# Two projection stages of the first layer issued to TensorE in a written order

## The chip, the cores and the metric

One core of one Trainium2 chip runs the whole program in one launch. The metric is the device time of that launch in microseconds (us); lower is better.

## What is computed

Two blocks of two layers each work on 1024 latent tokens and 256 context tokens of width 1024. The change concerns the first layer of the first block, which mixes the tokens in two ways side by side: a Fourier mix, and attention whose queries and keys pass through small latents (MLA).

```python
def mla_q(q_a, q_norm, w_qb, rope):
    q = (rmsnorm(q_a, q_norm) @ w_qb).reshape(b, n, MLA_HEADS, MLA_NOPE + MLA_ROPE)
...
def mla_kv(kv_a, k_pe, kv_norm, w_kvb, rope):
    kv = (rmsnorm(kv_a, kv_norm) @ w_kvb).reshape(b, n, MLA_HEADS, MLA_NOPE + MLA_V)
...
def even_layer(h_lat, h_ctx, w_in, q_norm, w_qb, kv_norm, w_kvb, w_out, rope, ctx_out):
    f_in, f_gate, q_a, kv_a, k_pe, m_gate = split_cols(h_lat @ w_in, EVEN_SPLITS)
...
    y_l = jnp.concatenate([fourier_mix(f_in) * jax.nn.silu(f_gate),
                           a_l.reshape(b, n, MLA_WIDTH) * jax.nn.silu(m_gate)], axis=-1) @ w_out
```

The query latent `q_a` has 384 columns, the key latent `kv_a` 256, the rotated key part `k_pe` 32, the Fourier input `f_in` 512. Both latents pass a root-mean-square norm over their columns before they meet the next weight.

## The kernel before: tiles, stages and order

All 1280 tokens lie in three chunks (`CH`): 0 and 1 of 512 latent tokens, 2 of 256 context tokens. Each product is made of three matmuls in a fast float format, high part by high part, low by high, high by low; so every operand exists as a high and a low tile (names that end in h and l). A weight block is loaded by `wblk` in chunks (`wraw`, issued on SP), its high part made by ScalarE (L161) and its low part by GpSimd (L169). `proj` (L236) loops over chunks and blocks of 128 output columns; its matmuls are recorded on L212. `dense_tok` gives tiles of 128 tokens instead; its matmuls are recorded on L224.

The order of the work on each engine is set by a scheduler that plays the program through a cost model before it is built; each engine then works its list strictly in that order. `in_order()` pins the matmuls issued inside it to the order in which they are written; outside of it the scheduler may interleave them. `later()` gives work a low priority, so that it fills holes of that model.

The stage in question is the function `e1`, between about 95 and 297 us of the profile:

1. The key latent's first two chunks and four token tiles of `f_in` (`u`), then its chunk 2. `normed_split` (L591) takes each finished tile of sums out of PSUM in three readings: ScalarE makes the high part (L600), VectorE the low part (L601), ScalarE the squares (L389 for the first block of 128 columns, L391 for the others); GpSimd adds the squares into `acck` (L392).
2. `rstd_cols` (L356) sums the squares over the columns by matmuls with a column of ones (L361); VectorE turns the sums into reciprocal roots by nine small operations (L363, L347 to L354). `bcast_cols` (L366) spreads these over all partitions by matmuls (L372) that ScalarE copies out (L374). Before, both stand together in `rstd_bc`, behind the key latent's chunk 2.
3. The other token tiles of `u`: six of the first half, ten of the second, which also carry `k_pe`; VectorE copies that part into `kp` twice (L674, L675). Transposes of `kp` (L683) and VectorE's table products (L685 to L691) make the rotated key part.
4. The keys: 12 tiles, each scaled out of PSUM by VectorE (L699). The values: 10 tiles, taken out by ScalarE.
5. The query latent: three blocks of 128 columns over three chunks (180 units of a 512-column matmul in all, a matmul of 256 columns counted as half a unit), into `accq`; then the sums and the spreading of all ten columns (`rstd_bc`), then the queries, 18 tiles of nine matmuls, scaled by VectorE (L728).
6. The Fourier mix (L834 on), whose VectorE part `fourier_in` (L799) is issued before the query latent: 18 additions on VectorE (L806 to L822) and 4 on GpSimd over ten `u` tiles, which SP loads back from memory.

Beside all of that runs `mod_rest` (L458) under `later()`: 32 loads (`wmt`, 512 KB each, two buffers) on SP, and on VectorE one or two products `wmj` (L477) per load. Its pool lies where the Fourier tiles go later, so SP's loads of the ten `u` tiles wait for the last `wmj`. Two gate tiles (24 matmuls each into the PSUM bank `f`) fill TensorE before the Fourier mix; VectorE's step on them is recorded on L385. PSUM has seven working banks (two `s`, one `o`, three `p`, one `g`) and the bank `f` for norms and gates.

Of the kernel before, what the change touches and what calls it, by code (L numbers as in the profile page):

```python
# [15 lines left out]
ALU = mybir.AluOpType  # L16
# [26 lines left out]
class Kern:  # L43
# [77 lines left out]
    def stg(self, n=512):  # L121
        return self.t(self.gp_, [P, 512], tag="stg", bufs=4)[:, 0:n]
# [497 lines left out]
    def e1(self):  # L620
        nc, A, V = self.nc, self.A, self.nc.vector
# [20 lines left out]
        KV = Act(2)  # L642
# [22 lines left out]
        for b, n in ((0, 256), (1, 288)):  # L665
            w = self.wblk(w_in, b * 256, n, pool=kvp) if b else wu
            for j in (0, 1, 2, 3, 8, 9, 4, 5, 6, 7) if b else (4, 5, 6, 7, 8, 9):
# [8 lines left out]
        for c, (a, b) in enumerate(CH):  # L676
            tab = self.t(kvp, [32, 2, 512], tag="kpe_tab", bufs=1)
            if c < 2:
                self.dma(tab, A["kpe_tab"][:, :, a:b])
            for e in range(2 if c < 2 else 1):  # L680
                s = self.sps()
                for j in range(a // P, b // P):
                    nc.tensor.transpose(s[0:32, j * P - a:j * P - a + P], kp[:, j, 32 * e:32 * e + 32], self.ident)  # L683
                if c == 2:
                    V.tensor_copy(kpe[:, a:b], s[0:32, 0:b - a])  # L685
                elif e == 0:
                    V.tensor_tensor(kpe[:, a:b], s[0:32], tab[:, 0], ALU.mult)
                else:
                    o = stg()[0:32]
                    V.tensor_tensor(o, s[0:32], tab[:, 1], ALU.mult)  # L690
                    V.tensor_tensor(kpe[:, a:b], kpe[:, a:b], o, ALU.add)  # L691
        self.dma(kpe_scr, kpe)
        w_kvb, w_qb = A["e_w_kvb"], A["e_w_qb"]
        w = self.wblk(w_kvb, 0, 512)

# [5 lines left out]
        self.proj(w, [(i * P, P, i) for i in range(4)], KV, ALLC, k_evac)  # L701
# [16 lines left out]
        w = self.wblk(w_in, 1056, 256)  # L718
# [24 lines left out]
        gs = self.open("e1g", side="right")  # L743
        gate, mix, todo = self.gate_evac(gate_scr, None, gs, 2), Act(), []
# [5 lines left out]
        def fill():  # L750
# [6 lines left out]
            for c in ALLC:  # L757
                for w, i in W:
                    yield from gates(w, i, c)
                todo.extend((k, c) for k in range(8))  # L760

# [22 lines left out]
        f, before = fill(), 0  # L784
# [1388 lines left out]
```

## Time and profile before

| | us |
|---|---|
| median of 3 runs | 2573.57 |
| lowest, highest | 2561.18, 2574.37 |
| the profiled execution | 2567.91 |
| its span in the trace | 2566.1 |

| engine | busy us | share of the span |
|---|---|---|
| TensorE (PE) | 2422.8 | 94% |
| VectorE (DVE) | 1685.4 | 66% |
| ScalarE (ACT) | 1127.3 | 44% |
| GpSimd (POOL) | 890.6 | 35% |

A busy share is an average over stages with different limits. PE is the engine to look at first, and the 6% of the span in which it does nothing are where an order can matter, together with the stretches in which its granted clock is at the half level after a pause.

### The profile page before, as it was taken

The numbers are of one execution on the slowest core, as the hardware profiler recorded it, in microseconds if no ns is written. First come the engines' busy times: TensorE is split into PE (matmuls) and PEld (weight loads), VectorE is DVE, ScalarE is ACT, GpSimd is POOL, SyncE is SP. The second block draws the span as 40 slices with busy tenths as digits, with TensorE's granted clock in tenths as the row PEclk, the third lists the DMA queues.
The fourth block names the chain that finished last, engine by engine and source line by source line (L and its number), as shares of the span: only waits on it lengthen the run. The fifth ranks groups of instructions, "written<-read, shape, count | busy, mean of one in ns | idle before, by whom it ended". The sixth has DMA issues, their size and how long they took to land. (4 is left out here: it accounts for less than half of the span.)

```text
span 2566.1 us, 36049 instructions
## 1 busy us (share of the span) xinstructions
PE 2422.8 (94%) x12814; PEld 1958.0 (76%) x12814; DVE 1685.4 (66%) x2983; ACT 1127.3 (44%) x2201; POOL 890.6 (35%) x750
## 2 busy tenths in 40 slices
PE   5999999999999999999898999999999999999998
PEld 3887777777678876766666779887877777799888
DVE  6785437788755648777776373547888577773455
ACT  3413226666652325655565233345655333513331
POOL 4204243354411152332322124145452243453231
PEclk7999999999999999999999999999999999999999
DMA  7476431132324231222323423233333332201433
GB/s 238 140 217 202 156 107 53 52 102 73 93 78 144 91 94 52 69 77 65 95 71 111 134 96 89 90 108 100 90 103 124 100 109 89 73 18 54 168 103 103
DMA packets 217092, 265.16 MB, mean 103 GB/s; under 512 B 42768, under 2 KB 142768, under 8 KB 216784
## 3 DMA queue, kind: packets, MB, share of 16 engines
q1 hardware_dynamic: 216192, 262.75, 32.9%
q8 instruction: 101, 1.65, 0.3%
q14 instruction: 79, 0.65, 0.1%
q10 hardware_dynamic: 720, 0.10, 0.0%
HBM read 188.60 MB, written 71.97 MB: 102 GB/s over the span
## 5 line engine op out<-in xcount | busy, mean ns | idle before, releaser
L169 POOL TENSOR_TENSOR wlo<-wraw,whi 128x512 fp32r<-128x512 f32 (+3 forms) x229 | 314.4, 1385 | 602.9 <-ACT whi L161 522.6
L169 DVE TENSOR_TENSOR pl<-pf,ph 128x512 fp32r<-128x512 f32 (+1 forms) x328 | 257.8, 787 | 80.3 <-ACT pf L957 41.0
L161 ACT ACTIVATE whi<-wraw 128x512 fp32r<-128x512 f32 (+3 forms) x261 | 154.5, 613 | 333.9 <-DMA wraw<-in_even_w_in 40.1
L957 ACT ACTIVATE ph<-s 128x512 fp32r<-128x512 f32 (+1 forms) x176 | 101.4, 576 | 107.4 <-PE s L954 106.7
L919 DVE TENSOR_REDUCE mx<-p 128x1 f32<-128x512 f32 (+1 forms) x208 | 116.8, 575 | 35.4 <-PE p L918 34.2
L1255 ACT ACTIVATE ph<-s 128x512 fp32r<-128x512 f32 x152 | 90.7, 597 | 107.6 <-PE s L1247 58.2
L212 PE MATMUL s<-ah,whi 128*128 128x512 f32 (+1 forms) x328 | 130.8, 399 | 5.6 <-ACT ah L493 3.2
L212 PE MATMUL s<-al,whi 128*128 128x512 f32 (+1 forms) x328 | 129.1, 394 | 1.8 <-DVE al L495 1.4
L212 PE MATMUL s<-ah,wlo 128*128 128x512 f32 (+1 forms) x328 | 129.4, 394 | 0.0
L212 PE MATMUL g<-ah,whi 128*128 128x512 f32 (+1 forms) x312 | 122.4, 392 | 3.4 <-DVE mixg L385 3.4
L212 PE MATMUL f<-ah,whi 128*128 128x512 f32 x304 | 123.7, 407 | 1.3 <-DVE stg L1368 0.8
L212 PE MATMUL f<-al,whi 128*128 128x512 f32 x304 | 123.0, 405 | 0.0
L212 PE MATMUL f<-ah,wlo 128*128 128x512 f32 x304 | 122.9, 404 | 0.0
L212 PE MATMUL g<-ah,wlo 128*128 128x512 f32 (+1 forms) x312 | 121.5, 390 | 0.0
L212 PE MATMUL g<-al,whi 128*128 128x512 f32 (+1 forms) x312 | 121.5, 390 | 0.0
L1621 DVE TENSOR_TENSOR_SCAN scu<-scu,ones_col 128x128 f32<-128x128 f32 (+3 forms) x64 | 97.1, 1531 | 14.1 <-ACT scu L1617 12.5
L1215 DVE CUSTOM_DVE_ANT_0 p<-p,maskt 128x384 f32<-128x384 f32 (+1 forms) x128 | 67.4, 530 | 58.0 <-PE p L1214 58.0
L957 ACT ACTIVATE pf<-s 128x512 f32<-128x512 f32 (+1 forms) x176 | 100.9, 573 | 2.0 <-DVE pl L169 1.8
L477 DVE CUSTOM_DVE_ANT_0 wmj<-wmt,srow,c_b_mod 128x1024 bf16<-128x1024 f32 x56 | 76.7, 1370 | 30.0 <-DMA wmt<-in_w_modT 27.7
L1255 ACT ACTIVATE pf<-s 128x512 f32<-128x512 f32 x152 | 90.2, 593 | 0.1
L212 PE MATMUL p<-ah,whi 128*128 128x512 f32 x224 | 89.5, 401 | 0.4 <-DVE x L1338 0.4
L212 PE MATMUL p<-al,whi 128*128 128x512 f32 x224 | 89.7, 400 | 0.0
(777 smaller groups left out, 7617.0 us busy)
## 6 DMA issues: line engine op xcount, KB each, us to landing
wmt<-in_w_modT SPq DMA_DIRECT2D x32, 512.0 KB
wraw<-in_even_w_in SPq DMA_DIRECT2D x56, 256.0 KB
wraw<-in_odd_w_in SPq DMA_DIRECT2D x48, 256.0 KB
wraw<-in_o_w_in SPq DMA_DIRECT2D x40, 256.0 KB
xold<-x_scr SPq DMA_DIRECT2D x40, 256.0 KB
mraw<-in_w_mod SPq DMA_DIRECT2D x16, 512.0 KB
x_scr<-x SPq DMA_DIRECT2D x32, 256.0 KB
mixx<-m_scr SPq DMA_DIRECT2D x30, 256.0 KB
```

Of the source, the lines that this page charges most:

```text
L161: nc.scalar.activation(out=out, in_=in_, func=AF.Copy)
L169: return e.tensor_tensor(out, in_, hi.bitcast(F32), ALU.subtract)
L212: self.nc.tensor.matmul(out, ws[:, k, c:c + m], a[k][ch], start=first and i == j == 0, stop=last and i == len(ks) - 1 and j == 2)
L477: V.tensor_tensor_reduce(out=junk, in0=w, in1=s[:, i], scale=0.5, scalar=self.bm[l][:, m, i:i + 1], op0=ALU.mult, op1=ALU.add, accum_out=s ...
L919: V.reduce_max(mx[:, e, j:j + 1], d[:, 0:y - x], axis=AX)
L957: nc.scalar.activation(out=t, in_=s, func=AF.Exp, scale=MLA_SCALE)
L1215: V.tensor_tensor_reduce(out=d[:, 0:n], in0=d[:, 0:n], in1=self.mask[:, off:off + n], scale=1.0, scalar=-3.0e38, op0=ALU.add, op1=ALU.max, ...
L1255: nc.scalar.activation(out=t, in_=s, func=AF.Exp, scale=0.125)
L1621: V.tensor_tensor_scan(out=rev, data0=rev, data1=self.ones.to_broadcast([P, n]), initial=1.0, op0=ALU.mult, op1=ALU.mult)
```

## The change

Key latent: the sums of the norm follow three token tiles of `u` later than they did, the spreading follows seven tiles behind the sums, and the transposes of `kp` are spread over the key tiles, two after each chunk. Everything from the first token tile to the last transpose is pinned in the written order.

Query latent: the third block of 128 columns (`w2`) no longer follows all of the first two but comes chunk by chunk, and its weights are loaded into the query pool. The norm is made chunk by chunk as well, with sums and spreading apart from each other and other matmuls between them; so there are three chains of nine small VectorE operations in place of one. The queries follow in pinned order, the third pair of blocks as before. The generator of the gate tiles is created earlier.

```diff
-        self.proj(wk, ((0, P, 0), (P, P, 1)), act, (2,), ev)
...
-        self.rstd_bc(rkb, acc, TT, 256.0, rkt)
...
+        with self.in_order():
+            u_proj(wu, 0, 256, (4,))
+            self.proj(wk, ((0, P, 0), (P, P, 1)), act, (2,), ev)
+            u_proj(wu, 0, 256, (5, 6))
+            self.rstd_cols(acc, TT // P, 256.0, rkt)
+            u_proj(wu, 0, 256, (7, 8, 9))
+            wu = self.wblk(w_in, 256, 288, pool=kvp)
+            u_proj(wu, 1, 288, (0, 1, 2, 3))
+            self.bcast_cols(rkt, TT // P, rkb)
+            u_proj(wu, 1, 288, (8, 9, 4, 5, 6, 7))
...
-        self.proj(w, [(i * P, P, i) for i in range(4)], KV, ALLC, k_evac)
+        with self.in_order():
+            for c in ALLC:
+                self.proj(w, [(i * P, P, i) for i in range(4)], KV, (c,), k_evac)
+                next(turns)
+                next(turns, None)
+            for _ in turns:
+                pass
...
         w = self.wblk(w_in, 1056, 256)
-        self.proj(w, ((0, P, 0), (P, P, 1)), act, ALLC, ev)
-        w = self.wblk(w_in, 1312, 128)
-        self.proj(w, ((0, P, 2),), act, ALLC, ev)
+        w2 = self.wblk(w_in, 1312, 128, pool=qp)
         rqb = acc
-        self.rstd_bc(rqb, acc, TT, 384.0)
+        first = {}
...
-        first = {}
-        for i in (4, 0, 2):
+        r = {c: self.t(qp, [P, (CH[c][1] - CH[c][0]) // P], nm=f"rq{c}") for c in ALLC}
+
+        def sums(c):
+            a, b = CH[c]
+            self.rstd_cols(acc[:, a:b], (b - a) // P, 384.0, r[c])
+
+        def spread(c):
+            a, b = CH[c]
+            self.bcast_cols(r[c], (b - a) // P, rqb[:, a:b])
+        first2, third = ((0, P, 0), (P, P, 1)), ((0, P, 2),)
+        with self.in_order():
+            self.proj(w, first2, act, (0,), ev)
+            self.proj(w2, third, act, (0,), ev)
+            self.proj(w, first2, act, (2,), ev)
+            sums(0)
+            self.proj(w2, third, act, (2,), ev)
+            self.proj(w, first2, act, (1,), ev)
+            spread(0)
+            sums(2)
+            self.proj(w2, third, act, (1,), ev)
+            spread(2)
+            w4 = self.wblk(w_qb, 4 * P, 256)
+            self.proj(w4, ((0, P, 4), (P, P, 5)), Q, (0,), q_evac)
+            sums(1)
+            self.proj(w4, ((0, P, 4), (P, P, 5)), Q, (2,), q_evac)
+            w0 = self.wblk(w_qb, 0, 256, pool=qp)
+            self.proj(w0, ((0, P, 0), (P, P, 1)), Q, (0, 2), q_evac)
+            spread(1)
+            self.proj(w4, ((0, P, 4), (P, P, 5)), Q, (1,), q_evac)
+            self.proj(w0, ((0, P, 0), (P, P, 1)), Q, (1,), q_evac)
+        for i in (2,):
```

Outside this stage the lists of all engines stay as they were but for single neighbours. What the scheduler makes of the change is seen at three places.

The first is on VectorE where the second half of `u` ends and the keys begin: the copies of `kp`, `mod_rest`'s products `wmj` (an ISA row each, with the read of its sum behind it) and the first scaled key tile. Before (L674 and L675 copy, L699 scales):

```order
L674 COPY kp_265_1094<-p_302_1551 128x32
L675 COPY kp_265_1094<-p_302_1551 128x32
L690 TENSOR_TENSOR stg_307_1594<-p_306_1589,kpe_tab_304_1581 32x512
L477 ISA wmj_194_620,mod1_110<-wmt_213_699,srow_192_618,c_b_mod1_614 128x1024
L477 ISA mod1_110 128x1
L685 COPY kpe_228_760<-s_313_1614 32x256
L691 TENSOR_TENSOR kpe_228_760<-kpe_228_760,stg_307_1594 32x512
L477 ISA wmj_194_620,mod1_110<-wmt_213_699,srow_192_618,c_b_mod1_614 128x1024
L477 ISA mod1_110 128x1
L687 TENSOR_TENSOR kpe_228_760<-g_309_1599,kpe_tab_308_1597 32x512
L690 TENSOR_TENSOR stg_311_1610<-s_310_1605,kpe_tab_308_1597 32x512
L699 TENSOR_TENSOR stg_319_1636<-o_318_1629,rkb_258_1055 128x512
```

With the change (L672 and L673 copy, L711 scales):

```order
L672 COPY kp_251_993<-o_300_1521 128x32
L673 COPY kp_251_993<-o_300_1521 128x32
L477 ISA wmj_194_620,mod1_110<-wmt_213_699,srow_192_618,c_b_mod1_614 128x1024
L477 ISA mod1_110 128x1
L477 ISA wmj_194_620,mod1_110<-wmt_214_703,srow_192_618,c_b_mod1_614 128x1024
L477 ISA mod1_110 128x1
L477 ISA wmj_194_620,mod1_110<-wmt_214_703,srow_192_618,c_b_mod1_614 128x1024
L477 ISA mod1_110 128x1
L672 COPY kp_251_993<-p_302_1551 128x32
L673 COPY kp_251_993<-p_302_1551 128x32
L711 TENSOR_TENSOR stg_309_1598<-p_308_1591,rkb_250_992 128x512
```

The last copy of `kp` and the first key tile stood behind the products of load 213 (the first key tile) and 212 (the copy); both now stand behind those of load 214, and the table products come after the first keys.

The second is on VectorE where `mod_rest` ends and `fourier_in` begins (fa and u tiles). Before:

```order
L601 SCALAR_TENSOR_TENSOR ql01_405_2088<-s_403_2062,c_e_q_norm_752,qh01_404_2087 128x512
L477 ISA wmj_194_620,mod1_110<-wmt_226_744,srow_192_618,c_b_mod1_614 128x1024
L477 ISA mod1_110 128x1
L601 SCALAR_TENSOR_TENSOR ql11_409_2119<-s_407_2093,c_e_q_norm_752,qh11_408_2118 128x512
L806 TENSOR_TENSOR fa0_376_1884<-u0_366_1864,u4_370_1868 128x512
L806 TENSOR_TENSOR fa1_377_1885<-u1_367_1865,u5_371_1869 128x512
L807 TENSOR_TENSOR u4_370_1868<-u0_366_1864,u4_370_1868 128x512
L806 TENSOR_TENSOR fa2_378_1886<-u2_368_1866,u6_372_1870 128x512
L807 TENSOR_TENSOR u5_371_1869<-u1_367_1865,u5_371_1869 128x512
L806 TENSOR_TENSOR fa3_379_1887<-u3_369_1867,u7_373_1871 128x512
L807 TENSOR_TENSOR u6_372_1870<-u2_368_1866,u6_372_1870 128x512
L601 SCALAR_TENSOR_TENSOR ql20_423_2185<-o_421_2159,c_e_q_norm_752,qh20_422_2184 128x512
```

With the change, at the end of `fourier_in` (L852 to L868 now), where the chain that makes chunk 0's reciprocal roots `rq0` (L363, L347 to L354) runs through it:

```order
L861 TENSOR_TENSOR fa1_377_1885<-u0_366_1864,u1_367_1865 128x512
L863 TENSOR_TENSOR fa3_379_1887<-u5_371_1869,u7_373_1871 128x512
L350 SCALAR_TENSOR_TENSOR rq0_397_1970<-rs_t_422_2138,rq0_397_1970 128x4
L865 SCALAR_TENSOR_TENSOR u0_366_1864<-fa2_378_1886,u4_370_1868 128x512
L866 SCALAR_TENSOR_TENSOR u1_367_1865<-fa2_378_1886,u4_370_1868 128x512
L867 SCALAR_TENSOR_TENSOR u5_371_1869<-fa3_379_1887,u6_372_1870 128x512
L868 SCALAR_TENSOR_TENSOR u7_373_1871<-fa3_379_1887,u6_372_1870 128x512
L351 TENSOR_TENSOR rs_t_422_2138<-rq0_397_1970 128x4
L601 SCALAR_TENSOR_TENSOR ql01_429_2205<-o_427_2179,c_e_q_norm_752,qh01_428_2204 128x512
L352 TENSOR_TENSOR rs_t_422_2138<-rs_t_422_2138,rs_s_421_2136 128x4
L353 SCALAR_TENSOR_TENSOR rs_t_422_2138<-rs_t_422_2138 128x4
L354 SCALAR_TENSOR_TENSOR rq0_397_1970<-rs_t_422_2138,rq0_397_1970 128x4
```

Before, no step of the norm stood among `fourier_in`'s; now `rq0` is finished three places behind its last addition. The third block's low part for chunk 0 (`ql20`), which stood eight places into `fourier_in`, now stands ahead of it.

The third is on SP, where the third block's weights (`wraw`, 128 columns, eight chunks of 64 KB in all) and `mod_rest`'s last loads alternate. Before:

```order
L128 DMA wmt_222_732<-in_w_modT 128x1024
L128 DMA wraw_417_2143<-in_e_w_in 128x128
L128 DMA wmt_223_735<-in_w_modT 128x1024
L128 DMA wraw_418_2147<-in_e_w_in 128x128
L128 DMA wraw_419_2151<-in_e_w_in 128x128
L128 DMA wmt_224_738<-in_w_modT 128x1024
L128 DMA wraw_420_2155<-in_e_w_in 128x128
L128 DMA wmt_225_741<-in_w_modT 128x1024
L128 DMA wraw_442_2296<-in_e_w_qb 128x256
L128 DMA wraw_443_2300<-in_e_w_qb 128x256
L128 DMA wmt_226_744<-in_w_modT 128x1024
```

With the change:

```order
L128 DMA wraw_391_1946<-in_e_w_in 128x128
L128 DMA wraw_392_1950<-in_e_w_in 128x128
L128 DMA wmt_224_738<-in_w_modT 128x1024
L128 DMA wmt_225_741<-in_w_modT 128x1024
L128 DMA wraw_393_1954<-in_e_w_in 128x128
L128 DMA wraw_394_1958<-in_e_w_in 128x128
L128 DMA wmt_226_744<-in_w_modT 128x1024
L128 DMA wraw_395_1962<-in_e_w_in 128x128
L128 DMA wraw_396_1966<-in_e_w_in 128x128
L128 DMA wraw_446_2300<-in_e_w_qb 128x256
L128 DMA u0_366_1864<-u_scr_73 128x512
```

The third block's last chunk still stands next to load 226, the last of `mod_rest`, though the block itself is now wanted right behind the first two blocks of chunk 0.

## Rows read from the trace of the kernel before

**Rows 1.** Windows: busy time of each engine in two stretches of the stage.

```profile
core 0: us, PE busy (x) PEld busy (x) DVE busy (x) ACT busy (x) POOL busy (x), PEclk, DMA share, GB/s
95.00:182.00 87.00, 80.13 (x582) 76.35 (x581) 74.01 (x134) 19.47 (x41) 16.05 (x9) 0.98 0.65 202
...
240.00:290.00 50.00, 44.09 (x220) 37.43 (x220) 31.94 (x48) 8.78 (x19) 24.77 (x21) 0.90 0.37 118
```

**Rows 2.** Waits of PE from 95 to 345 us: total, times, longest.

```profile
PE f L361 <- POOL accq L392: 4.9, 1, 4.9
PE f L372 <- DVE rkt L354: 3.1, 1, 3.1
PE f L212 <- DVE gst L385: 2.3, 1, 2.3
PE g L683 <- DVE kp L674: 1.7, 1, 1.7
...
PE p L212 <- DVE kpe L687: 1.3, 1, 1.3
PE f L372 <- ACT accq L374: 0.7, 1, 0.7
```

**Rows 3.** Windows again: the three stretches at the half clock.

```profile
132.20:135.60 3.40, 3.40 (x16) 3.40 (x17) 2.69 (x6) 0.60 (x1) 0.00 (x0) 0.50 0.86 261
241.40:251.70 10.30, 7.50 (x23) 6.34 (x24) 10.30 (x12) 2.52 (x6) 8.47 (x7) 0.50 0.18 51
292.60:296.00 3.40, 3.40 (x19) 3.40 (x18) 0.00 (x0) 0.00 (x0) 0.00 (x0) 0.50 0.94 336
```

**Rows 4.** Timeline of DVE, 165 to 188 us: start, length, instruction, idle before.

```profile
165.92 1.28 DVE L477 CUSTOM_DVE_ANT_0 wmj<-wmt,srow,c_b_mod 128x1024 bf16<-128x1024 f32 x1 [0.25 <-DMA wmt<-in_w_modT]
...
169.06 0.17 DVE L674 COPY kp<-p 128x32 f32<-128x32 f32 x1
...
174.40 0.67 DVE L699 TENSOR_TENSOR stg<-o,rkb 128x512 f32<-128x512 f32 x1
...
187.60 0.68 DVE L699 TENSOR_TENSOR stg<-g,rkb 128x512 f32<-128x512 f32 x1
```

**Rows 5.** Timeline of SP's queue: two loads of mod_rest, then the u tiles.

```profile
162.23 0.33 SPq L128 DMA_DIRECT2D wmt<-in_w_modT  x1
...
221.94 0.38 SPq L128 DMA_DIRECT2D wmt<-in_w_modT  x1
227.60 4.71 SPq L128 DMA_DIRECT2D u<-u_scr  x10
```

**Rows 6.** Timeline of DVE, 226 to 257 us.

```profile
226.28 1.28 DVE L477 CUSTOM_DVE_ANT_0 wmj<-wmt,srow,c_b_mod 128x1024 bf16<-128x1024 f32 x1 [2.31 <-DMA wmt<-in_w_modT]
...
233.68 1.29 DVE L806 TENSOR_TENSOR fa<-u,u 128x512 f32<-128x512 f32 x2 [5.44 <-DMA u<-u_scr]
234.90 0.68 DVE L807 TENSOR_TENSOR u<-u,u 128x512 f32<-128x512 f32 x1
...
239.01 0.74 DVE L601 SCALAR_TENSOR_TENSOR ql<-o,c_e_q_norm,qh 128x512 fp32r<-128x512 f32 x1
...
244.62 1.21 DVE L816 TENSOR_TENSOR fa<-u,u 128x512 f32<-128x512 f32 x1
...
251.52 0.74 DVE L601 SCALAR_TENSOR_TENSOR ql<-p,c_e_q_norm,qh 128x512 fp32r<-128x512 f32 x1
257.06 0.17 DVE L363 TENSOR_SCALAR rs_s<-f 128x10 f32<-128x10 f32 x1 [4.81 <-PE f L361]
```

**Rows 7.** Timelines of PE, four rows from 195 to 297 us.

```profile
195.78 0.39 PE L212 MATMUL p<-ah,whi 128*128 128x512 f32 x1
...
237.80 0.39 PE L212 MATMUL p<-qh,whi 128*128 128x512 f32 x1
...
244.20 1.23 PE L361 MATMUL f<-ones_col,accq 128*128 128x1 f32 x5 [4.86 <-POOL accq L392]
...
296.41 0.67 PE L846 MATMUL o<-c_f_tw,fa 128*128 128x256 f32 x2
```

More of the change, by code (lines that the diff above doesn't have):

```diff
@@ L659, in e1, with u_proj @@
             self.dma(u_scr[j * 256:(j + 1) * 256, 0:256].rearrange("(e p) n -> p e n", p=P), t.rearrange("p (e n) -> p e n", e=2))
-        self.proj(wk, ((0, P, 0), (P, P, 1)), act, (2,), ev)
         rkt = self.t(kvp, [P, 10], nm="rkt")
         rkb = self.t(kvp, [P, TT], nm="rkb")
-        self.rstd_bc(rkb, acc, TT, 256.0, rkt)
         kp = self.t(kvp, [P, 10, 64], nm="kp")
-        for b, n in ((0, 256), (1, 288)):
-            w = self.wblk(w_in, b * 256, n, pool=kvp) if b else wu
-            for j in (0, 1, 2, 3, 8, 9, 4, 5, 6, 7) if b else (4, 5, 6, 7, 8, 9):
+        def u_proj(w, b, n, js):
+            for j in js:
                 s = self.sps()[:, 0:n]
@@ L675, in e1 @@
                     V.tensor_copy(kp[:, j, 32:64].rearrange("p (a b) -> p a b", a=2), s[:, 256:288].rearrange("p (a b) -> p a b", a=2)[:, ::-1, :])
[L676 to L691, printed above, removed]
@@ L692, in e1, with rotate_kpe @@
-        self.dma(kpe_scr, kpe)
+        def rotate_kpe():
+            for c, (a, b) in enumerate(CH):
+                tab = self.t(kvp, [32, 2, 512], tag="kpe_tab", bufs=1)
+                if c < 2:
+                    self.dma(tab, A["kpe_tab"][:, :, a:b])
+                for e in range(2 if c < 2 else 1):
+                    s = self.sps()
+                    for j in range(a // P, b // P):
+                        nc.tensor.transpose(s[0:32, j * P - a:j * P - a + P], kp[:, j, 32 * e:32 * e + 32], self.ident)
+                    if c == 2:
+                        V.tensor_copy(kpe[:, a:b], s[0:32, 0:b - a])
+                    elif e == 0:
+                        V.tensor_tensor(kpe[:, a:b], s[0:32], tab[:, 0], ALU.mult)
+                    else:
+                        o = stg()[0:32]
+                        V.tensor_tensor(o, s[0:32], tab[:, 1], ALU.mult)
+                        V.tensor_tensor(kpe[:, a:b], kpe[:, a:b], o, ALU.add)
+                    yield
+            self.dma(kpe_scr, kpe)
@@ L694, in e1 @@
         w = self.wblk(w_kvb, 0, 512)
+        turns = rotate_kpe()
         def k_evac(i, c, ps):
@@ L717, in e1, with gates, fill @@
         ev = self.normed_split(qp, "q", Q, gq, acc, sm)
+        gate = self.gate_evac(gate_scr)
+        def gates(w, i, c):
+            for e in (0, 1):
+                yield from self.dense_steps(w, e * P, act, c, self.FT, lambda ps: gate(i + e, c, ps))
+        def fill():
+            for i, c0 in ((0, 544), (2, 800)):
+                w = self.wblk(w_in, c0, 256)
+                for c in ALLC:
+                    yield from gates(w, i, c)
+            W = [(self.wblk(w_in, c0, 256), i) for i, c0 in ((4, 1696), (6, 1952))]
+            for c in ALLC:
+                for w, i in W:
+                    yield from gates(w, i, c)
+                todo.extend((k, c) for k in range(8))
+        f, before = fill(), 0
         w = self.wblk(w_in, 1056, 256)
-        self.proj(w, ((0, P, 0), (P, P, 1)), act, ALLC, ev)
-        w = self.wblk(w_in, 1312, 128)
-        self.proj(w, ((0, P, 2),), act, ALLC, ev)
+        w2 = self.wblk(w_in, 1312, 128, pool=qp)
         rqb = acc
-        self.rstd_bc(rqb, acc, TT, 384.0)
+        first = {}
         def q_evac(i, c, ps):
@@ L744, in e1 @@
         gate, mix, todo = self.gate_evac(gate_scr, None, gs, 2), Act(), []
-        def gates(w, i, c):
-            for e in (0, 1):
-                yield from self.dense_steps(w, e * P, act, c, self.FT, lambda ps: gate(i + e, c, ps))
-        def fill():
-            for i, c0 in ((0, 544), (2, 800)):
-                w = self.wblk(w_in, c0, 256)
-                for c in ALLC:
-                    yield from gates(w, i, c)
-            W = [(self.wblk(w_in, c0, 256), i) for i, c0 in ((4, 1696), (6, 1952))]
[L757 to L760, printed above, removed]
         def add():
@@ L783, in e1 @@
         am_scr = dram("am_scr", [512, TT])
-        f, before = fill(), 0
         with self.later():
```

## The prediction

> **What bounds the kernel now.** TensorE (PE) is busy for 94% of the span, so a change of order can win back only its waits and the stretches at the half clock. I read the waits of PE over the stage first. Those that the new order can reach are two for sums or roots of a norm, 4.9 and 3.1 us, two around the rotated key part, 1.7 and 1.3, and one for a spread, 0.7 [rows 2]: 11.7 us. Then I read the granted clock. Behind the wait of 3.1 us lie 3.4 us at 0.50, which is 1.2 GHz, all busy; around that of 4.9 us the clock is 0.50 for 10.3 us, of which PE worked 7.5 [rows 3]. Work at the half level takes twice its time, so the loss is 1.7 and 3.75 us. Together that is 17.1 us, the most the change can give.
>
> The windows then show who else is busy. From 95 to 182 us VectorE (DVE) worked 74.0 of 87 us, from 240 to 290 us 31.9 of 50 [rows 1]. So in the first part PE's order is not free: DVE has to follow. The timeline of DVE says what sets its pace. A `mod_rest` load issued at 162.23 [rows 5] is used at 165.92 [rows 4], 3.7 us later, and its two products take 1.3 us each. With two buffers, and each load issued once the products on its buffer are over, two loads go through per 3.7 + 2.6 = 6.3 us. The copies of `kp` and the keys stand in the same list, at fixed places among these products.
>
> **Key part.** Work on PE and the other engines stays the same; only places change. The waits of 3.1 (with 1.7 of clock), 1.7 and 1.3 us go: -7.8 us on PE. But PE's gain there is not kept. Before, the first key tile on DVE followed load 213 and ran at 174.40 [rows 4], with most of the rotation done. Now it follows load 214. Load 212 is used at 165.92, so by the pace above 214 is used at 172.2 and its products end at 174.9; with two copies the first key runs at about 175.2, however early PE is. PE then fills the seven PSUM banks and waits. From first to last key DVE took 13.9 us (174.40 to the end of the row at 187.60). Now the whole rotation stands behind the first key too: four table products of about 0.6 us and a copy of 0.35 that used to come before, 2.75 us, and two products of 1.3. So the last key ends at about 194.5 in place of 188.3, 6 us later, and the query latent starts on PE at about 202 in place of 195.78 [rows 7]. The bounds: 196 if the keys don't hold PE at all, 206 if PE adds a wait of its own at the sums, whose last square now has GpSimd's weight split ahead of it; I take 202, as it follows from the list.
>
> The Trainium skill, page "DMA: Bandwidth & Descriptors", section "Anatomy of one DMA — SWDGE (gpsimd) path", gives 2.0 us and the bytes at 436 GB/s, for a load from another queue than ours; for 512 KB that would be an estimate of 3.2 us. The row has 3.7 us, so here the trace differs; by 3.2 us the pace would be 0.5 us quicker per two loads, and the last of `mod_rest` about 3 us earlier.
>
> **Query part, what goes.** Before, PE waited 4.9 us for GpSimd's last squares, because the third block's low part `ql20` stood eight places into `fourier_in`, which itself waited for the `u` tiles until 233.68; `ql20` came at 239.01 [rows 6]. In the new list it stands ahead, so this wait goes with its clock loss: -8.6 us, and -0.7 for the spread.
>
> **Query part, what comes.** PE needs `rq0` for the first spread. The third block, chunk 0, comes right behind the first two, but SP sends its last chunks beside load 226. The 180 units took 42.0 us (195.78 to 237.80, [rows 7]), 0.233 each; the third block's chunk 0 could end 72 units on, at 218.8, its last weights are in at about 221: a wait of about 2.5 us. At 156 units, 36.4 us, plus 0.5 for four sums, PE reaches the spread at about 241.
>
> On DVE `rq0` ends behind `fourier_in`, and that waits for the `u` tiles. The last `wmj` ended 53.2 us behind the first key (174.40 to 227.56, [rows 4, 6]), 13 loads. Now 12 are left. At the quick pace, 3.2 us a load, with 4 us of rotation beside, that is 42 us, with nothing gained 53; I take the middle, 48, so the last `wmj` is over at 223 (217 to 228). From there to `fourier_in` it was 6.1 us (227.56 to 233.68); `fourier_in` with two low parts took 17.8 us (233.68 to 251.52, [rows 6]). Now there are three low parts and nine small steps in it, of 0.17 us each by the row at 257.06: 19.4 us. So `rq0` is ready at 223 + 6.1 + 19.4 = 248.5 (242.5 to 254). PE waits there some 7 us: the old wait comes back at another matmul. The 18 further small steps of the other chains, 3 us, lie beside matmuls, since DVE is idle for 18 of 50 us in that stretch [rows 1]; without this cover the next spreads would be 3 us later.
>
> **The sum.** From 237.80 to the Fourier mix at 296.41 PE took 58.6 us [rows 7]. Without the waits of 4.9, 0.7 and 2.3 us and the clock losses of 3.75 and 1.7 (the third stretch of [rows 3]) this is 45.3 us of work. Behind the first spread PE has this to do, plus the third block's chunk 1, 24 units or 5.6 us, less four sums (0.5; five took 1.23 at the half clock), and I leave 1 us for the Fourier tables, which are still sent behind the queries' stores: 51.4 us. So the Fourier mix starts where it did if `rq0` is ready at 245.0. It is ready at 248.5: +3.5 us. To that comes the clock behind a 7 us wait, between the 1.7 and 3.75 us of the two rows; 2.5: **+6 us**. Beyond the Fourier mix the lists are unchanged, so this stays. The profiled execution took 2567.91 us, which gives 2574; it lies 5.7 us under the median, and on the median's scale it is 2579. The forecast's own ends are -2.5 (242.5, no clock loss) and +12.8 (254 and 3.75): 2571 to 2586. About 0.5%, 12.9 us, is what a measurement here can tell from no change.
>
> **Rivals** (times on the median's scale).
> *A small gain.* `rq0` is ready before PE gets there, so PE alone sets the end of the stage: 241 - 245.0 = -4 us, 2570. For it: several of `fourier_in`'s steps took 1.21 us and others of the same size 0.68 [rows 6], with GpSimd busy 8.5 of 10.3 us there [rows 3]; ten such steps at 0.68 would give 5 us, and a last product at the early bound the rest. Against it: GpSimd has the same splits and its own four Fourier steps there as before. The Trainium skill, page "SBUF — State Buffer", section "SBUF: two separate sides", says that DVE and GpSimd share a pair of ports under an exclusive lock; by that rule these slow steps go wherever GpSimd is idle, and the trace agrees in that they lie where it is busy.
> *Faster.* DVE's list does not hold the keys or the roots, and the whole 17.1 us come, less a wait of 3 us at the first sums: -14 us, 2559. It decides where the first spread is reached by 231 and finds `rq0`. Against it stands the row at 233.68: `fourier_in` cannot start before the `u` tiles, and these wait for all of `mod_rest`.
> *Slower.* The third block's chunks, among `mod_rest`'s last loads, hold these back. Load 226 was used 4.3 us after its issue (221.94 to 226.28). If one such wait is added to a `mod_rest` that gains nothing, its end is 175.2 + 53.2 + 4.3 = 232.7 and `rq0` comes at 258.2: 13.2 us late, with 3.75 of clock +17 us, 2591. It decides from `rq0` at 254. Against it: as many chunks lay among these loads before.
>
> **How the numbers follow.** Forecast 0.55; small gain 0.20; faster 0.13; slower 0.12. The first two are within 0.5%, so faster 0.13, same 0.75, slower 0.12. The range goes from 2562 (below the small gain, as the runs themselves differ by that) to 2589, and leaves out the faster case and the far end of the slower one.
>
> **What would show it.** Right: PE's waits for `rkt`, `kp` and `kpe` are gone, the first key on DVE comes near 175, the first query-latent matmul near 202, the last `wmj` near 223, and PE's longest wait in the stage is the first spread for `rq0`, 5 to 9 us, with half clock behind it; the Fourier mix starts near 302. Wrong: no such wait, the query latent starts before 198, or the Fourier mix starts before 290 or behind 310; a difference behind the Fourier mix would make all of it wrong.

## The result, and the profile after

Over eight runs of each kernel the changed one takes 2589.56 us (median; 2580.66 to 2597.01) and the one before 2573.97 us: ratio 1.0062, 95% interval 1.0046 to 1.0078, or +15.6 us. The forecast was +6 us, 2579, about no change. The two profiled executions, 2580.66 and 2567.91 us, differ by 12.8.

The head of the page of after answers to the table of busy times: PE has the work that it had, to 0.5 us, and stands idle longer; DVE is busy 7.5 us more.

```profile
span 2578.9 us, 36077 instructions
...
PE 2422.3 (94%) x12814; PEld 1956.5 (76%) x12814; DVE 1692.9 (66%) x3001; ACT 1128.1 (44%) x2201; POOL 893.3 (35%) x750
```

Waits of PE from 95 to 345 us after, the view of [rows 2]:

```profile
engine line waited for: us in total, times, longest us
PE p L212 <- ACT whi L161: 4.4, 3, 1.8
PE f L372 <- DVE rq L354: 4.3, 1, 4.3
PE o L892 <- DMA c_f_cs<-in_f_cs: 3.7, 1, 3.7
PE p L212 <- DVE kp L673: 3.6, 1, 3.6
PE o L683 <- DVE kp L673: 1.6, 1, 1.6
...
PE s L683 <- DVE kpe L687: 1.0, 1, 1.0
```

The wait of 4.9 us for `accq` and that for `rkt` are gone, as forecast. New are three of about 4 us: for the weights of the third block (`whi`), for the first chunk's roots (`rq`), and for the Fourier tables. The waits around the rotated key part (`kp`, `kpe`) were forecast to go, and did not: they total 6.2 us where [rows 2] have 3.0.

Timeline of DVE after, to be read against [rows 4, 6]; the last number is the idle time before a row:

```profile
172.35 0.68 DVE L711 TENSOR_TENSOR stg<-p,rkb 128x512 f32<-128x512 f32 x1
...
219.89 1.28 DVE L477 CUSTOM_DVE_ANT_0 wmj<-wmt,srow,c_b_mod 128x1024 bf16<-128x1024 f32 x1 [2.04 <-DMA wmt<-in_w_modT]
...
228.67 1.33 DVE L852 TENSOR_TENSOR fa<-u,u 128x512 f32<-128x512 f32 x2 [2.06 <-DMA u<-u_scr]
...
234.58 1.25 DVE L347 TENSOR_SCALAR rq<-rs_s 128x4 int32<-128x4 int32 x1
...
244.62 1.23 DVE L351 TENSOR_TENSOR rs_t<-rq 128x4 f32<-128x4 f32 x1
...
246.44 0.64 DVE L352 TENSOR_TENSOR rs_t<-rs_t,rs_s 128x4 f32<-128x4 f32 x1
...
247.31 0.16 DVE L354 SCALAR_TENSOR_TENSOR rq<-rs_t,rq 128x4 f32<-128x4 f32 x1
```

Timeline of GpSimd after, beside the last of these rows:

```profile
243.57 2.26 POOL L869 TENSOR_TENSOR fa<-u,u 128x512 f32<-128x512 f32 x1 [3.18 <-DVE u L866]
245.79 1.26 POOL L870 TENSOR_TENSOR fa<-u,u 128x512 f32<-128x512 f32 x1
```

Timeline of PE after, the rows that answer to [rows 7]:

```profile
199.53 0.40 PE L212 MATMUL p<-ah,whi 128*128 128x512 f32 x1
...
247.62 1.19 PE L372 MATMUL f<-c_ident,rq 128*128 128x128 f32 x4 [4.27 <-DVE rq L354]
...
301.37 0.67 PE L892 MATMUL o<-c_f_tw,fa 128*128 128x256 f32 x2 [3.69 <-DMA c_f_cs<-in_f_cs]
```

| step | forecast, us | after, us |
|---|---|---|
| first key on DVE | 175.2 | 172.35 |
| first matmul of the query latent | 202 | 199.53 |
| last `wmj` over | 223 | 221.17 |
| wait for the third block's weights | 2.5 | 4.4 |
| `fourier_in` starts | 229.1 | 228.67 |
| `rq0` ready | 248.5 | 247.47 |
| PE reaches the first spread, waits | 241, 7 | 243.35, 4.27 |
| wait for the Fourier tables | 1 | 3.69 |
| Fourier mix starts | 302 | 301.37 |

So the chain up to `rq0` ran as forecast, each time within 3 us. But the mix starts at 301.37 with one of the two gate tiles still to do, and with a pause just before it. Timelines of PE show the second gate tile (`ach`). Its last matmul before stands ahead of the mix at 296.41:

```profile
296.13 0.27 PE L212 MATMUL f<-ach,wlo 128*128 128x256 f32 x1
```

Its first matmul after stands behind the start of the mix:

```profile
307.26 0.47 PE L212 MATMUL f<-ach,whi 128*128 128x256 f32 x1
```

SP's queue shows where the tables stand: behind stores of the queries, and with them 5.0 us later than before. Before:

```profile
279.49 11.10 SPq L128 DMA_DIRECT2D q_scr<-stg  x12
290.79 0.33 SPq L128 DMA_DIRECT2D c_f_tw<-in_f_tw  x1
```

After:

```profile
291.39 4.32 SPq L128 DMA_DIRECT2D q_scr<-stg  x5
295.81 0.37 SPq L128 DMA_DIRECT2D c_f_tw<-in_f_tw  x1
```

Two windows of after, in the columns of [rows 3]: behind the wait for `rq`, and behind that for the tables, the granted clock is near the half level for most of the time.

```profile
246.90:254.70 7.80, 6.25 (x20) 5.30 (x21) 3.04 (x13) 1.91 (x4) 1.43 (x2) 0.56 0.00 0
301.40:305.40 4.00, 4.00 (x12) 3.22 (x13) 0.63 (x2) 1.93 (x4) 0.32 (x1) 0.60 0.55 197
```

**Where the time comes up.** ScalarE works the same list in both kernels but for a few places, so the starts of its same instructions, subtracted, give the lag of one trace against another. Of the two traces after lags 5.0 us at the mix, 9.5 at 412 us, 6.2 at 1254, and then steps to 12.4 by 1302, near which it stays (12.8 at the end). A step 1 ms behind the edit was not in the forecast at all. There the lists had changed too: the scheduler plays the whole program, and with a new first layer other instructions were the next to be free. On GpSimd a product of an attention tile with its reciprocals (`gatt`) now stands ahead of the next unit's queries (`qq`); on SP and DVE some loads of `am_scr` and the squares on them stand elsewhere. Timelines of GpSimd and DVE after, at this place:

```profile
1279.06 0.74 POOL L1337 TENSOR_TENSOR gatt<-gatt,grb 128x256 f32<-128x256 f32 x1 [5.13 <-DMA grb<-rec_scr]
1279.77 0.61 POOL L163 TENSOR_SCALAR qq<-raw 64x512 fp32r<-64x512 f32 x1
...
1281.61 0.69 DVE L1163 TENSOR_TENSOR stg<-stg,stg 128x512 f32<-128x512 f32 x1 [3.63 <-DMA stg<-am_scr]
...
1286.97 0.69 DVE L1163 TENSOR_TENSOR stg<-stg,stg 128x512 f32<-128x512 f32 x1 [3.73 <-DMA stg<-am_scr]
```

In the trace of before, GpSimd's split of `qq` waits for no such load, and DVE's waits for `am_scr` near there are 1.4 and 0.5 us. DVE has the low part of `qq` to make behind these waits, and PE waits for it once more, some 20 us behind a long wait for `qq` (8.6 us) that before has too (8.7). Before has no such second wait there. PE after:

```profile
1291.74 0.58 PE L1260 MATMUL p<-kk,qq 128*128 128x256 f32 x1 [5.10 <-DVE qq L169]
```

### The profile page after: what moved, and what is told of

Read it like the earlier page. It is cut to its first block, busy times and chain, and to the rows that moved or that the text cites. A ratio compares the mean times of both kernels' runs of the same rounds, so it can differ in the third digit from the quotient of the medians.

```text
span 2578.9 us, 36077 instructions
## 1 busy us (share of the span) xinstructions
PE 2422.3 (94%) x12814; PEld 1956.5 (76%) x12814; DVE 1692.9 (66%) x3001; ACT 1128.1 (44%) x2201; POOL 893.3 (35%) x750
## 5 line engine op out<-in xcount | busy, mean ns | idle before, releaser
L212 PE MATMUL s<-ah,whi 128*128 128x512 f32 (+1 forms) x312 | 124.5, 399 | 5.1 <-ACT ah L493 3.2
L212 PE MATMUL s<-al,whi 128*128 128x512 f32 (+1 forms) x312 | 122.9, 394 | 1.8 <-DVE al L495 1.4
L212 PE MATMUL s<-ah,wlo 128*128 128x512 f32 (+1 forms) x312 | 123.2, 395 | 0.0
L212 PE MATMUL p<-ah,whi 128*128 128x512 f32 x240 | 96.9, 405 | 4.4 <-ACT whi L161 4.4
L212 PE MATMUL p<-ah,wlo 128*128 128x512 f32 x240 | 96.1, 404 | 1.4 <-POOL wlo L169 1.3
L212 PE MATMUL p<-al,whi 128*128 128x512 f32 x240 | 96.6, 402 | 0.0
```

Of the source, the lines that this page charges most:

```text
L212: self.nc.tensor.matmul(out, ws[:, k, c:c + m], a[k][ch], start=first and i == j == 0, stop=last and i == len(ks) - 1 and j == 2)
```

## The experiments

Theory A: the loss is in two parts. In the first layer `rq0` ends behind `fourier_in`, and beside it the late weights and tables; behind it the re-ordered lists at 1270 to 1300 us cost by themselves. The rivals are in each expectation. "Step" is the growth of a trace's lag from 1254 to 1302 us against the kernel before, in its second execution. Ratios are to the kernel before in runs of the same chip; its medians there were 2569.6 to 2571.7.

### Which part of the change, which part of the program

**The stage new, the lists behind it old.** Matmuls that nobody reads shift the scheduler's clock until the lists at 1270 us are again those of before. First eight of them ahead of the windowed attention, at 945 us:

```diff
+        extra = self.sps("f")
+        for _ in range(8):
+            nc.tensor.matmul(extra[:, 0:128], self.ident, self.ident, start=True, stop=True)
```

> The changed kernel with eight spare matmuls of 128 columns ahead of the windowed attention of the second layer; they shift the scheduler's model so that the lists of DVE, POOL and SP around that attention come out as in the kernel before (two swaps of neighbours on DVE elsewhere). Theory A (the loss has two parts: about 9.5 us in the first layer, and about 6 us a millisecond later where those lists changed): the 6 us are gone, ratio to before 1.003 to 1.005, 2582 to 2587 us, and no wait of PE for qq near 1280 us. Theory B (the 6 us there are a chance of one profiled execution, all of the loss lies in the first layer): the same as the changed kernel, 1.006, 2590 us. The spare matmuls themselves should cost at most 1 us.

Measured: 2589.12 us, ratio 1.0074 (1.0052 to 1.0096). A miss. In its trace the step is 0.9 us, but the time did not fall.

**The stage old, the lists behind it new**: the same with 16 such matmuls, in the kernel before.

> The kernel before with sixteen spare matmuls of 128 columns at the same place; the lists of the first layer stay those of before, and around the windowed attention DVE, POOL and SP get word for word the lists of the changed kernel. Theory A: the second part of the loss alone, 5 to 8 us with the spare matmuls (at most 2 us), ratio 1.002 to 1.003, 2579 to 2582 us, and PE waits some 5 us for qq near 1275 us. Theory B: no more than the spare matmuls, ratio up to 1.001, and no such wait.

Measured: 2579.16 us, 1.0031 (1.0017 to 1.0045), step 3.6 us. By the number a hit, but the spare matmuls alone are 3.7 us of the 8, read in its trace, and PE's second wait for `qq`, at 1285 us, is there with 3.7.

**The key part alone**, with the query part of before.

> The new order of the key latent and the keys, the query latent as before; the lists behind the first layer are those of before. Theory A (the query part carries the loss; the key part delays the query latent by 4 us but ends mod_rest some 6 us earlier, so the u tiles and with them the old wait of 4.9 us and its clock loss go): 1 to 5 us faster, 2569 to 2573 us, first query-latent matmul near 199.5 us. Rival C (the key part is the loser, since DVE and not PE sets the pace there): 3 to 6 us slower, 2577 to 2580 us.

Measured: 2572.58 us, 1.0007 (0.9993 to 1.0021). Neither A's gain nor C's loss is there: PE waits 4.0 us for `kp`, and a wait of 4.1 us for `accq` remains.

**The query part alone**, with the key part of before.

> The key part as before, the query latent chunk by chunk. Its lists around the windowed attention are nearly those of the changed kernel. Theory A: query latent from 195.8 us, the last wmj near 227.5 us, fourier_in from 233.7 us and rq0 near 252.5 us, where PE is at about 240 us: a wait of 9 to 13 us with 4 to 5 us of clock loss behind it, so 13 to 18 us in the first layer and 6 us later, 2593 to 2598 us. Rival C (the key part is the loser): the first layer loses 5 us or less, 2579 to 2585 us with the later part.

Measured: 2576.92 us, 1.0024 (1.0008 to 1.0040). A miss for both, and an instructive one: here the scheduler put the first chain ahead of `fourier_in` by itself (all but its last step, which stands behind the first addition, at 233.84 us), and there is no wait for it. The weights are still in eight loads, and the waits for `whi` (4.2 us) and the tables (2.9) are there. So the chain's place is not in the written order; in the two kernels it comes out differently from the same written query part.

**The changed kernel again**, as the base for what follows:

> The changed kernel once more, unedited, so that the next three have it on the same chip. Ratio to before 1.005 to 1.008. If the wait of PE for qq near 1280 us is a matter of the lists and not of chance, it is in this profile too, 4 to 6 us long.

Measured: 2588.83 us, 1.0060 (1.0042 to 1.0078); waits of 4.2 us for `rq`, 4.9 for `whi`, 4.3 for the tables. The time is as expected, and the second wait for `qq` is there, but with 2.0 us and not 4 to 6.

**The first layer exactly as changed, all lists behind it exactly those of before**, by six spare matmuls at 1196 us (1.5 us in the trace).

> As the first run, but with six spare matmuls inside the windowed attention (at its third group of keys), which give DVE, ACT, POOL and SP behind the first layer exactly the lists of before. Theory A (9.5 us in the first layer, 6 us at the windowed attention): 5 to 6 us under the changed kernel beside it, ratio to before 1.003 to 1.005. Theory B (all of the loss in the first layer; the lists later cost nothing): the same as the changed kernel beside it, within 2 us.

Measured: 2585.06 us, 1.0050 (1.0033 to 1.0067): 3.8 us under the changed kernel, between the two theories, with intervals that overlap.

### Taking the waits of the first layer away

**The roots of chunk 0 ahead of the Fourier input.**

```diff
-        Z = self.fourier_in(self.open("fourA", side="left"), u_scr)
+        fourA = self.open("fourA", side="left")
...
-            sums(0)
+            with self.in_order(mybir.EngineType.DVE):
+                sums(0)
+                Z = self.fourier_in(fourA, u_scr)
```

> The changed kernel with DVE's order pinned so that the nine steps that make rq0 stand ahead of fourier_in; SP's list and the lists behind the first layer are those of the changed kernel. Theory A (the first spread waits for rq0 behind fourier_in): that wait of 4.3 us and its clock loss are gone, the Fourier mix starts 4 to 6 us earlier, 4 to 6 us under the changed kernel beside it. Rival D (the stage's end is set by loads: the third block's weights and the Fourier tables): the wait moves to these, less than 2 us under the changed kernel.

Measured: 2577.03 us, 1.0027 (1.0009 to 1.0046): 11.8 us under the changed kernel, twice what A said. Its waits of PE in the stage:

```profile
PE p L212 <- ACT whi L161: 5.0, 3, 2.3
PE o L894 <- DMA c_f_cs<-in_f_cs: 2.5, 1, 2.5
PE p L212 <- DVE kp L673: 2.0, 1, 2.0
PE f L372 <- DVE rq L354: 1.9, 1, 1.9
```

The first spread waits for nothing; the 1.9 us are at a later one.

**The third block's weights in two loads instead of eight.**

```diff
-        step = max(1, kt * n // 512 // 2)
+        step = 4 if n == 128 else max(1, kt * n // 512 // 2)
```

> The changed kernel with the third block's weights loaded in two chunks of 256 KB in place of eight of 64 KB, so that SP sends both ahead of mod_rest's last seven loads; in the lists that follow, the nine steps of rq0 also stand ahead of fourier_in. The lists at the windowed attention are close to those of before (POOL's are the same, DVE has some neighbours swapped). Theory A: the waits for the third block's weights (4.4 us) and for rq0 (4.3 us) are both gone, the first layer loses 1 us or less against before, ratio to before 0.998 to 1.002. Rival C (the key part carries the first layer's loss): still 4 us or more behind, ratio 1.002 to 1.005.

Measured: 2572.97 us, 1.0002 (0.9987 to 1.0016). In the median all of the loss is gone, by one line. (Its one trace still lags by 5.0 us at 412 us; and the later lists moved with it: GpSimd's are again those of before, so that this run does not part the first layer from what lies behind it.) The waits for `whi` and for `rq` are both gone, since the first chain now stands ahead of `fourier_in` (ready at 228.6 us). Waits of PE:

```profile
PE o L892 <- DMA c_f_twc<-in_f_twc: 3.8, 1, 3.8
PE f L361 <- ACT accq L374: 3.4, 1, 3.4
PE p L212 <- DVE kp L673: 3.2, 1, 3.2
```

**The same two loads in the kernel before**, as a control:

> A control: the kernel before with the third block's weights in two chunks and nothing else. Theory A: there the third block comes last and its weights were never waited for, so only mod_rest's last loads can come a little earlier: ratio 0.999 to 1.000. If the two chunks by themselves were the gain of the runs above (rival), 0.996 to 0.998.

Measured: 2568.86 us, 1.0003 (0.9986 to 1.0019). By itself the edit gives nothing; its worth lies in what waits behind these loads.

### Looking for a version that beats both

**The key part of before, the query part of the change, two loads.**

> The key part as before, the query latent chunk by chunk as in the change, its third block's weights in two chunks of 256 KB; the nine steps of rq0 stand ahead of fourier_in, and the lists behind the first layer are those of before. Theory A (the change loses by rq0, by the late weights and by the lists later, while its query part itself removes the old wait): no wait for weights or rq0, the Fourier mix starts 3 to 7 us earlier than in the kernel before, ratio to before 0.997 to 0.999. Rival E (what the query part gains is taken back by the Fourier tables and the other loads): ratio 0.9995 to 1.001.

Measured: 2570.82 us, 0.9999 (0.9986 to 1.0013). No gain; the mix starts at 293.80, 2.6 to 3.0 us earlier than before. The first spread is free, and the wait has moved to the second, whose chain stands behind `fourier_in` now. Timeline of PE:

```profile
231.65 1.05 PE L372 MATMUL f<-c_ident,rq 128*128 128x128 f32 x8
249.61 1.19 PE L372 MATMUL f<-c_ident,rq 128*128 128x128 f32 x4 [9.61 <-DVE rq L354]
```

**The same, and the chains of chunks 0 and 2 both ahead of `fourier_in`.**

> The key part of before, the query part of the change with the third block's weights in two loads, and now the roots of chunk 0 and those of chunk 2 both ahead of the Fourier input's additions on VectorE; ten spare matmuls at the windowed attention (under 1 us) bring VectorE's, GpSimd's and SyncE's lists behind the first layer back to those of before. Theory A (the wait of 9.6 us at the second spread came from the chain of chunk 2 standing behind the Fourier input): that wait is gone or under 3 us, the Fourier mix starts near 286 to 289 instead of 293.8, and the ratio to before is 0.996 to 0.998. Rival E (the wait moves on once more, to the spread of chunk 1, whose chain lies in the Fourier input, or to the Fourier tables): a wait of 5 us or more at one of these two, the Fourier mix at 292 or later, ratio 0.999 to 1.001.

Measured: 2580.59 us, 1.0038 (1.0022 to 1.0055). Rival E by its mechanism, as the wait moved on to the third spread, that of chunk 1; the time lies above both ranges. The ten spare matmuls took 2.4 us, more than expected. Timeline of PE:

```profile
232.62 1.05 PE L372 MATMUL f<-c_ident,rq 128*128 128x128 f32 x8
240.55 0.61 PE L372 MATMUL f<-c_ident,rq 128*128 128x128 f32 x4
264.19 2.04 PE L372 MATMUL f<-c_ident,rq 128*128 128x128 f32 x8 [4.92 <-DVE rq L354]
```

**The gate tiles pinned behind the queries**, to cover the wait for the tables, in the kernel with the query part and two loads (the run at 2570.82 us).

> As the run before, with the gate tiles pinned right behind the queries, so that two of them stand between the last query and the Fourier mix and cover the load of its tables; eight spare matmuls in the windowed attention keep DVE, POOL and SP there as before (ACT has two neighbours swapped). Theory A: PE's wait for the tables (3.7 us in the changed kernel) is gone; 2 to 4 us under the run before, ratio to before 0.995 to 0.998. If the tables are no bound of their own (rival), the same as the run before.

Measured: 2600.04 us, 1.0119 (1.0096 to 1.0142). The wait for the tables is gone, but PE waits where the attention starts, which it does not without the pinning. That the two tiles are missing there is a reading that no run tests. One row of its waits, 345 to 480 us:

```profile
PE p L948 <- POOL qh L163: 19.1, 1, 19.1
```

### The lists a millisecond later

**The kernel before once more**, one execution, as the base of the lags:

> The kernel before, unedited, for one more profile of it on this chip: the Fourier mix starts within 2 us of 296.4 us, and the time from there to the end agrees with the first profile within 5 us.

Measured: 2574.13 us. The mix starts at 296.78; from there to the end it is 5.8 us longer than the first execution of the same kernel, so two executions part by more than the 5 us expected.

**The first layer of the run with two chains, without its spare matmuls.** In this kernel SP's and DVE's lists at 1270 us are changed; GpSimd's turned out to be that of before, other than expected below.

> The same first layer without the spare matmuls; VectorE's, GpSimd's and SyncE's lists at 1270 to 1300 us are then changed against those of before, as they are in the changed kernel (one product of GpSimd ahead of another, some loads and some squares of the windowed attention in another order). Theory A (these lists cost some 4 us a millisecond behind the stage): 3 to 5 us more than the run with the spare matmuls, a ratio higher by 0.001 to 0.002, with the step between 1237 and 1317 us in the two traces. Rival C (the lists cost nothing; what the profiles show there is difference between executions): equal within 1 us, or less by the spare matmuls' part of a microsecond.

Measured: 2571.49 us, 1.0001 (0.9985 to 1.0017), step 1.3 us. A's sign was wrong: this kernel is 9 us quicker than its sister with the old lists (2580.59), of which the spare matmuls are 2.4.

**GpSimd's one swap alone**, in the kernel before (a dependency of the split on the product), and undone in the changed kernel (the product issued behind the split):

```diff
...
         self.hi(qq[0:64], raw, "pool")
+        if (kv, blk) == (3, 0):
+            self.tc.add_manual_dep(nc.cur_bb.bb.instructions[-1], self.product.name, mybir.DependencyInfo(mybir.DependencyClass.NoSync, mybir.DependencyReason.DATA))
...
```

> The kernel before, with a single change of order: on GpSimd the last product of one attention tile with its reciprocals (gatt, which waits for its DMA) stands ahead of the split of the next unit's queries (qq), as in the changed kernel; SyncE's and VectorE's lists are those of before. Theory A (this one swap is what costs at 1254 to 1302 us): PE's waits for qq there are some 2 to 5 us longer, the step between 1254 and 1302 us is 3 to 5 us, and the ratio to before is 1.001 to 1.002. Rival F (it takes the re-ordered loads and squares on SyncE and VectorE as well, or the difference is one between executions): step within 2 us, ratio within 0.0007 of 1.

> The changed kernel with that one swap undone: the product of GpSimd is issued behind the split of the next queries, as in the kernel before; the first layer and nearly all of SyncE's and VectorE's lists are those of the changed kernel. Theory A: the step between 1254 and 1302 us is gone (under 2 us), and the time is 3 to 5 us under the changed kernel's 2588.8 to 2589.6, a ratio to before of 1.004 to 1.0050. Rival F: the step stays above 3 us and the ratio at 1.0055 to 1.0065.

Measured: 2571.75 us, 0.9998 (0.9980 to 1.0017), step 1.1; and 2589.51 us, 1.0057 (1.0037 to 1.0078), step 1.7. The first is rival F: the swap alone costs nothing that can be measured. In the second the step went, as A said, and the time did not, as F said.

### The lags side by side

Lag in us against the kernel before in its one execution above, at four times of that trace (starts of the same ScalarE instructions subtracted):

| kernel | at 412 | at 1254 | at 1302 | at 2525 | ratio |
|---|---|---|---|---|---|
| before, first profile | 1.4 | -2.7 | -4.6 | -5.7 | 1 |
| before, one swap | -0.8 | -8.9 | -7.8 | -7.2 | 0.9998 |
| before, lists of after | 0.0 | -1.4 | 2.2 | 6.9 | 1.0031 |
| changed | 10.9 | 3.5 | 7.8 | 7.1 | 1.0062 |
| changed, again | 11.8 | 7.0 | 11.6 | 19.0 | 1.0060 |
| changed, 8 spare matmuls | 10.6 | 4.4 | 5.3 | 12.0 | 1.0074 |
| changed, lists of before | 13.4 | 5.1 | 6.0 | 11.2 | 1.0050 |
| changed, swap undone | 12.1 | 7.7 | 9.4 | 12.3 | 1.0057 |
| changed, roots first | 5.9 | -1.7 | 3.0 | 5.3 | 1.0027 |
| changed, two loads | 5.0 | 2.7 | 4.8 | 4.4 | 1.0002 |
| query part, two loads | -0.1 | -0.1 | 0.5 | 0.2 | 0.9999 |
| the same, two chains | 1.3 | 4.4 | 5.4 | 10.3 | 1.0038 |
| two chains, no spare matmuls | 5.6 | 0.9 | 2.2 | 5.8 | 1.0001 |
| key part alone | 3.6 | 1.8 | 1.0 | 0.7 | 1.0007 |
| query part alone | 3.5 | -3.2 | -2.3 | -3.2 | 1.0024 |
| before, two loads | -3.4 | -11.7 | -11.4 | -10.4 | 1.0003 |
| gate tiles pinned | 20.6 | 17.2 | 18.7 | 24.9 | 1.0119 |

At 412 us the five profiles with the changed first layer lie at 10.6 to 13.4, mean 11.8; the four with that of before (its base, 0, among them) at -0.8 to 1.4, mean 0.2. So **the first layer costs 11.6 us of the 15.6**, and no profile of one group comes near the other. Further on executions blur this: the two means are 8.8 apart at 1254 and 13.8 at 2525 us. From 1254 to 1302 us the four kernels with all of the new lists (changed, changed again, roots first, lists of after) step by 3.6 to 4.7 us, every other one by -1.9 to 2.1. PE's second wait for `qq`, between 1285 and 1296 us, is 5.1, 2.0, 2.6 and 3.7 us in these four, and 1.2 or less there in the others. So the step goes with the new lists as a whole, and neither with GpSimd's swap alone nor with the rest alone. Whether it lasts to the end can't be told: behind 1302 us two executions of the changed kernel differ by 8 us. The kernels without the step took 2585.06, 2589.12 and 2589.51 us, the changed one 2588.83 and 2589.56.

## Why the prediction was wrong

The forecast was +6 us, and +15.6 were measured. Of the 9.6 us between them 5.6 lie in the first layer, where the sum ends at the start of the Fourier mix, with too little for its tables and nothing for a gate tile that had slid behind that start (3). The other 4.0 come up behind the first layer, against "so this stays" (5), and what makes them is open.

1. **Key part: right in what sets the pace, wrong in a sign.** DVE's list sets the keys, and PE's gain there came back as waits for `kp`, which the text had named as gone; the query latent starts 3.75 us later than before (forecast: 6). Alone the part makes no difference that can be measured.
2. **`rq0` behind `fourier_in`: right.** (Its 19.4 us leave out the third low part; `fourier_in` up to `rq0` took 18.8.) The wait came at the first spread, 4.27 us instead of 7, as PE came there some 2 us later than forecast. In the five profiles of this first layer the spread starts at 247.62 to 250.15, right behind `rq0`, and the mix at 301.37 to 304.50. PE's waits there were 4.3 (changed), 4.2 (again), 4.2 (lists of before), 2.2 (8 spare matmuls) and 2.3 (swap undone): in the last two PE had worked about 10 us at the half level around 222 us (granted clock 0.72 from 214 to 232 us, against 1.00 in the others) and came later, and lost nothing by it (lags of 10.6 and 12.1 at 412 us, among the five). With the roots first the lag at 412 us falls from 11.8 to 5.9, by these rows: 2.3 us of the wait (4.2, less the 1.9 at a later spread), 1.8 at the tables (4.3 to 2.5), and 3.0 of the clock (in the windows at granted clock 0.50 or 0.51 PE worked 6.0 and 3.4 us at the half level behind the two waits, a loss of 4.7, and 3.4 behind the later spread, a loss of 1.7), less a new wait of 1.4 for a gate tile. The medians differ by 11.8; the second half of that lies behind the first layer and is not explained.
3. **"and I leave 1 us for the Fourier tables": mis-sized, and the end of the sum misplaced.** The tables took 3.7 to 5.0 us in the five profiles of the changed first layer, with half clock behind. And the mix starts at 301.37 with a gate tile still to do, 24 matmuls of half a unit of 0.233 us, 2.8 us, which before stood ahead of it. So it is luck that the mix starts near the forecast's 302: the longer wait and the missing tile cancel. The sum's +6, less 1.0 for `rq0` ready at 247.47 and not 248.5, plus 2.7 and 2.8 for these two terms, makes 10.5; the first profiles of the two kernels have 9.5, the mean of five 11.6. Sending the tables ahead of the stores was not tried.
4. **The wait for the third block's weights, 2.5: mis-sized**, at 4.4 us, and 1.6 to 4.9 in the other four profiles. In the sum it moved only PE's arrival at the spread, which did not bind. But in this kernel these loads also go with the first chain's place behind `fourier_in`: with two loads both waits are gone, and so, in the median, is the loss.
5. **"Beyond the Fourier mix the lists are unchanged, so this stays": wrong.** They were changed at 1270 to 1300 us, and there the changed kernel's trace steps by 6.2 us against the first one of before, and by 4.3 and 4.6 in its two profiles against the second. Single neighbours had changed places, and the text took that for no change, though it named a difference behind the mix as what would make all of it wrong. How much of the step stays to the end is open, as said.
6. **The rivals.** The slower one had the right price, +17 us, by luck: its mechanism was not there, as `mod_rest` was not held back (its last product was over at 221.17 us, against 227.56 in [rows 6]). Faster fell as the first spread was reached at 243.35 and not by 231, and the small gain as `rq0` came 4 us behind that. The slow steps on which the small gain rested were there again: the row at 244.62 is a 128x4 step of 1.23 us that ends, within 0.03 us, where GpSimd's row from 243.57 does; the one at 246.44 ends where GpSimd's next one does; and the one at 247.31, as small, with GpSimd idle, took 0.16. The Trainium skill, page "SBUF — State Buffer", section "SBUF: two separate sides", says that DVE and GpSimd share a pair of ports under an exclusive lock; the trace agrees in these three rows.

## What to carry to other kernels

A small chain that another engine waits for takes the place in its own engine's list that the scheduler finds for it; pinning TensorE's order does not pin VectorE's. So ask of each such chain what large work it may fall behind, and what late load may go with that: here two loads in place of eight, and the lists that followed, made 15.9 us. When one chain is moved ahead, look which chain is now the last; and ask of work that is moved to fill a wait what it covered where it stood. Where a scheduler plays the whole program, compare the lists to the end of it before calling anything unchanged.

## What the runs showed that was not expected

Executions of one kernel differ by as much as the parts of this change are worth: the 120 runs of the kernel before beside these experiments have a median of 2570.4 us and a standard deviation of 4.7. Stretches at the half clock come and go. From 2246 to 2270 us the first execution of the changed kernel had a granted clock of 1.00; the second, in the window view with the columns of [rows 3], had 0.79:

```profile
2246.00:2270.00 24.00, 21.59 (x95) 18.33 (x93) 17.72 (x20) 6.54 (x8) 13.23 (x7) 0.79 0.29 98
```

Over this place the two executions part by 4.8 us.

Two kernels that differ by ten spare matmuls at 942 us (2.4 us) and a few exchanged rows of SP and DVE stand 9 us apart in their medians, with intervals that don't meet. The first layer's traces don't show it (lags of 1.3 and 5.6 us at 412, in the other direction). Its cause is open; so is what puts the changed kernel's medians 15.6 to 18 us above before where the first layer has 11.6. Not tried: all three chains ahead of `fourier_in`.
